# Moving one modulation block of layer 1 from the first attention to the handover behind the first expert stage

## The chip, the cores and the metric

The kernel runs on one core of a Trainium2 chip as one launch. The metric is the device time of that launch in microseconds (us). Three runs of the kernel before took 3518.69, 3520.12 and 3525.53 us; the median is 3520.12. TensorE (PE) multiplies matrices, VectorE (DVE), ScalarE (ACT) and GpSimd (POOL) do elementwise work, SyncE (SP) issues most of the transfers (DMAs).

## What is computed

Two transformers of two layers each run one behind the other on 512 tokens of width 1024 (and 256 context tokens in the first). All numbers are float32. Of the first:

```python
for l in range(2):
    mod_l = silu(c) @ w_ada[l] + b_ada[l]            # 6 x 1024 numbers; mod_c likewise from c_ctx
    sh1, sc1, g1, sh2, sc2, g2 = split(mod_l, 6)
    h = rmsnorm(x, norm_mix[l]) * (1 + sc1) + sh1    # ctx likewise, with mod_c
    o = mixer_ab(h) if l == 0 else mixer_na(h)       # two kinds of attention
    x = x + g1 * o
    h = rmsnorm(x, norm_ffn[l]) * (1 + sc2) + sh2
    x = x + g2 * hier_moe(h)                         # 32 experts, each token goes to 2
x = rmsnorm(x, norm_final)                           # then the second transformer
```

The modulation vectors depend on `c` and `c_ctx` alone, so each can be computed at any time before its first use. A modulation block here is 2048 columns of one layer's `w_ada`. Block (1, 1) is columns 2048 to 4095 of layer 1: the gate `g1` and the shift `sh2`. Both are first used behind layer 1's attention (called NA).

## The kernel before, in words

Stages run in this order: start and projections, the first attention, its output projection and the router, the first expert stage, the first handover, the norm and turn of the NA input, the NA attention, the second expert stage, the second handover, and the second transformer. A scheduler places instructions in each engine's queue; an engine works through its queue strictly in that order, and a weight load takes the next slot of a ring (`wraw`, a 512 KB load issued by SP). A slot is free again when its last reader is done.

**Modulation blocks.** `ada_pieces(l, b, ...)` gives eight steps, k = 0 to 7. Each issues two 512 KB loads of `w_ada` and four matmuls, one for each quarter of the columns, which add into one PSUM bank `ad` (L405); `cc` is the silu of `c` and `c_ctx`. A matmul in float32 shows as two records in the trace. Behind step 7, DVE adds the bias and POOL writes the result to the buffer `mod` with two DMAs. Five blocks (two of layer 0, three of layer 1) make 40 steps, which `mixer_ab` spreads evenly over the 96 groups of the first attention.

**Expert stage.** `moe` and `experts` run 32 experts one after another. An expert's weights are 12 loads (gate and up 8, down 4). Its tokens are transposed (L1284), multiplied by gate and up (`ex_in`, L1275, `ea<-wr,xT`), passed through the activation (`sg`, L1297 and L1298), transposed again (L1308), copied out by DVE (`aT`, L1309), multiplied by down (L1275, `ea<-wr,aT`), scaled on DVE by the token's weight and gain (`ey`, L1319 and L1320) and scattered to the buffer `Y` by POOL (L1321). `ex_arms` is the branch that does this for 64 tokens, or for 128 if the expert has more. L1319 in layer 0 writes `ey`, so it waits until the earlier scatter that reads the same buffer has landed.

**Overflow block.** An expert with more tokens than 128 gets a further block. With these inputs one such block runs in layer 0 and none in layer 1. `overflow` issues its 12 loads from inside the loop, then the first loads of the next stage (`then`, here `na_w_in`); the block itself runs behind the loop (L1146 and L1147), and behind it a loop for still more blocks (L1149) that doesn't run.

**Handover.** `gains` spreads a row of gains over 128 partitions (`spread`, L441 and L442), 32 records on PE in layer 0; before, this stands ahead of the overflow block. Then ACT loads a function table and casts the next stage's weights (`wh<-wr`), SP loads the rows of `Y` (`yp`), and for each tile DVE adds them into `xO`, ACT and DVE form the normed `h`, and PE transposes it. `warm` is a run of matmuls whose result nobody reads; `warm(ps, xO[:, 0, 0:512], 6)` stands at the first tile of the first handover, one on `xO[:, 2]` in the second handover.

Of the kernel before, what the change touches and what calls it, by code (L numbers as in the profile page):

```python
# [8 lines left out]
F32 = mybir.dt.float32  # L9
# [5 lines left out]
ALU = mybir.AluOpType  # L15
# [4 lines left out]
P = 128  # L20
# [46 lines left out]
class Ker:  # L67
# [320 lines left out]
    def ada_pieces(self, l, b, ap, ps, tag, keep=None):  # L388

        nc = self.nc  # L390
        c0 = b * 2048
        g = {}

        def tile(k):
            if k == 0:
                g["a"] = ps.tile([P, 512], F32, name="ad", tag=tag, bufs=3 if tag == "pt" else None)
                g["b"] = ap.tile([P, 512], F32, name="adab", tag="adab", bufs=1)
                nc.gpsimd.memset(g["b"], 0.0)
                for who in range(2):
                    nc.gpsimd.dma_start(self.quarters(g["b"], who), self.I["b_ada"][l, c0:c0 + 2048].rearrange("(j n) -> j n", j=4))  # L400
# [6 lines left out]
            if k == 7:  # L407
                nc.vector.tensor_add(g["b"], g["b"], g["a"])
                if keep is not None:
                    keep.append(g["b"])  # L410
                    return
                for who in range(2):
                    nc.gpsimd.dma_start(self.mod[l, who, c0:c0 + 2048].rearrange("(j n) -> j n", j=4), self.quarters(g["b"], who))
        return [lambda k=k: tile(k) for k in range(8)]
# [171 lines left out]
    def mixer_ab(self, xO, begin=None):  # L586
# [8 lines left out]
        with ExitStack() as eo:  # L595
# [139 lines left out]
            with ExitStack() as e3:  # L735
# [105 lines left out]
                for b in range(3):  # L841
                    ada += self.ada_pieces(1, b, pp, ps, "pt")
# [13 lines left out]
            with ExitStack() as e1:  # L856
                pp = e1.enter_context(self.pool(name="abp", bufs=1))
                ps = e1.enter_context(self.pool(name="abps6", bufs=3, space=PSUM))
                self.weights(e1, 8, 0, "right")
# [221 lines left out]
    def moe(self, l, xO, t0, nt, who_of, sc=None, then=()):  # L1081
# [12 lines left out]
        with ExitStack() as e1:  # L1094
# [14 lines left out]
            pg = e3.enter_context(self.pool(name=f"mg{l}", bufs=1, side="right"))  # L1109
            px = e1.enter_context(self.pool(name=f"mx{l}", bufs=2, side="right"))  # L1110
            ps = e1.enter_context(self.pool(name=f"mqs{l}", bufs=8, space=PSUM))
# [23 lines left out]
            def overflow():  # L1135
# [8 lines left out]
            nov, w = self.experts(l, tix, idx, wl, ctx, xg, hD, Y, T, px, ps,  # L1144
                                  [first] + past + ([] if l else [self.shift_scale]), gains, overflow)
# [155 lines left out]
    def ex_out(self, w, sg, h, idx, wl, Y, T, px, ps):  # L1301
# [30 lines left out]
    def experts(self, l, tix, idx, wl, ctx, xg, hD, Y, T, px, ps, past, gains, overflow):  # L1332
# [6 lines left out]
        a = ps.tile([P, 512], F32, name="ea", tag="b")  # L1339
        self.ex_in(a, w, x, 0, range(2))  # L1340
        for e in range(NE):
# [13 lines left out]
            if e + 1 < NE:  # L1355
                a = ps.tile([P, 512], F32, name="ea", tag="b")
                self.ex_in(a, w1, x1, 0, range(2))
# [4 lines left out]
        gains()  # L1362
# [35 lines left out]
    def table(self, fn):  # L1398

        t = self.sm.tile([P, 1], F32, name="tab")  # L1400
# [10 lines left out]
    def mixer_na(self, xO, begin=None, finish=None):  # L1411
# [13 lines left out]
        with ExitStack() as e1:  # L1425
# [3 lines left out]
            with ExitStack() as e2:  # L1429
# [23 lines left out]
                with ExitStack() as e3:  # L1453
                    ps = e3.enter_context(self.pool(name="naps", bufs=8, space=PSUM))
# [3 lines left out]
                    with self.pinned():  # L1458
# [32 lines left out]
                        for t in range(NT + 2):  # L1491
# [4 lines left out]
                            if add and t == 0:  # L1496
                                self.warm(ps, xO[:, 0, 0:512], 6)
# [127 lines left out]
            with ExitStack() as e2:  # L1625
                self.halves(e2, 8, "right")
# [110 lines left out]
    def even_mixer(self, xO, normed=False, finish=None):  # L1737
# [3 lines left out]
        with ExitStack() as e1:  # L1741
            OT = xO[:, 4:6, :].rearrange("p a (b n) -> p (a b) n", n=512)
            with ExitStack() as e2:
# [8 lines left out]
                with ExitStack() as e3:  # L1752
# [46 lines left out]
                    else:  # L1799
# [6 lines left out]
                        self.warm(ps, xO[:, 2, 0:512], 6)  # L1806
# [141 lines left out]
    def conv_ffn(self, l, xO, dst=None):  # L1948
        nc, tc, I = self.nc, self.tc, self.I
        wu, wd = I["ffn_w_up_2"][l], I["ffn_w_down_2"][l]  # L1950
        with ExitStack() as e1:
            ph = e1.enter_context(self.pool(name=f"ff{l}", bufs=1))
# [362 lines left out]
```

## Time and profile before

| | us |
|---|---|
| median of three runs | 3520.12 |
| the profiled execution | 3519.27 |
| its span | 3517.5 |
| mean granted clock of TensorE | 0.977 |
| first attention, 200 to 490: PE busy | 283.57 |
| first expert stage, 612 to 1150: PE busy | 496.25 |
| first handover, 1150 to 1213: PE busy | 37.54 |
| second handover, 2140 to 2220: PE busy | 67.53 |

The span is the time between the first and the last instruction of the profile; 1.77 us of the profiled time lie around it. [...] In a row of a timeline, what stands in brackets is the idle time of the engine ahead of it and what ended it.

### The profile page before, as it was taken

How to read it: one execution, taken by the hardware profiler on the slowest of the kernel's cores; microseconds unless marked ns; L12 is line 12 of the kernel's file. 1: busy time of each engine (PE TensorE's matmuls, PEld its weight loads, DVE VectorE, ACT ScalarE, POOL GpSimd, SP SyncE). 2: the span in 40 equal slices, each digit the busy share in tenths (PEclk: the TensorE clock that was granted, in tenths of full speed). 3: DMA queues.
4: the chain of work that ended last, by engine and by line, in shares of the span. 5: the costliest groups of instructions: out<-in, count | busy, mean ns of one | idle time of the engine just before them, and what ended most of it. 6: DMA issues, size and time to landing. Idle time of an engine off the chain costs nothing. (4 is left out here: it accounts for less than half of the span.)

```text
span 3517.5 us, 44393 instructions
## 1 busy us (share of the span) xinstructions
PE 3270.0 (93%) x16460; PEld 2118.1 (60%) x16460; DVE 1515.1 (43%) x2899; ACT 1027.7 (29%) x1908; POOL 468.3 (13%) x569
## 2 busy tenths in 40 slices
PE   7999998999988699998988888998999999999998
PEld 5954556333322387765332234876888888788887
DVE  3476565222222356565211114527443456455344
ACT  3475541100000144441000002326332334333232
POOL 1044421111111023331111110103000000000000
PEclk9999999999999899999999999999999999999999
DMA  5134465798999622236999996322333354233331
GB/s 202 49 119 133 166 217 196 306 417 329 352 410 397 229 73 75 69 113 226 416 408 399 402 397 244 122 91 85 96 96 96 84 66 95 70 99 105 96 97 48
DMA packets 350859, 676.34 MB, mean 192 GB/s; under 512 B 42804, under 2 KB 194548, under 8 KB 349184
## 3 DMA queue, kind: packets, MB, share of 16 engines
q1 hardware_dynamic: 313816, 626.50, 50.6%
q0 software_dynamic: 17360, 25.94, 2.1%
q10 hardware_dynamic: 19416, 20.34, 1.8%
q8 instruction: 168, 2.75, 0.3%
q14 instruction: 99, 0.81, 0.1%
HBM read 676.22 MB, written 29.19 MB: 201 GB/s over the span
## 5 line engine op out<-in xcount | busy, mean ns | idle before, releaser
L1275 PE MATMUL ea<-wr,xT 128*64 128x512 f32 x2336 | 607.5, 601 | 38.5 <-DMA wr<-in_moe_w_up_dram 21.8
L157 DVE TENSOR_TENSOR wh<-wr,wh 128x1024 fp32r<-128x1024 f32 (+2 forms) x269 | 328.8, 1228 | 308.9 <-ACT wh L156 308.2
L240 PE MATMUL aw<-hh,wh 128*128 128x512 f32 (+1 forms) x1184 | 432.1, 366 | 2.9 <-ACT wh L156 2.6
L241 PE MATMUL aw<-hl,wh 128*128 128x512 f32 (+1 forms) x1184 | 432.7, 366 | 0.0
L242 PE MATMUL aw<-hh,wh 128*128 128x512 f32 (+1 forms) x1184 | 431.4, 365 | 0.0
L1275 PEld LDWEIGHTS ea<-wr,xT 128*64 128x64 f32 x2336 | 178.9, 137 | 408.9 <-issue 293.5
L156 ACT CAST wh<-wr 128x1024 fp32r<-128x1024 f32 (+2 forms) x269 | 274.2, 1027 | 417.6 <-PE acc L242 287.4
L1275 PE MATMUL ea<-wr,aT 128*64 128x512 f32 x1168 | 284.4, 632 | 53.0 <-DVE aT L1309 43.5
L240 PEld LDWEIGHTS aw<-hh,wh 128*128 128x128 f32 x1184 | 223.9, 189 | 39.7 <-ACT wh L156 3.5
L241 PEld LDWEIGHTS aw<-hl,wh 128*128 128x128 f32 x1184 | 224.3, 189 | 38.3 <-issue 3.5
L242 PEld LDWEIGHTS aw<-hh,wh 128*128 128x128 f32 x1184 | 224.1, 189 | 37.6 <-issue 3.5
L510 POOL TENSOR_TENSOR pp<-pp,rc 128x768 f32<-128x768 f32 (+3 forms) x192 | 211.0, 1106 | 260.0 <-DVE rc L509 247.3
L1285 ACT COPY xT<-pt 128x512 f32<-128x512 f32 x65 | 38.1, 586 | 683.8 <-PE pt L1284 672.9
L1275 PEld LDWEIGHTS ea<-wr,aT 128*64 128x64 f32 x1168 | 82.7, 144 | 200.1 <-issue 136.6
L1321 POOL DMA_INDIRECT Y<-ey,idx x73 | 73.1, 1001 | 848.3 <-DVE ey L1320 767.2
L508 ACT ACTIVATE pp<-s,nm 128x768 f32<-128x768 f32 (+3 forms) x192 | 137.1, 716 | 157.4 <-DVE nm L1593 81.1
L240 PE MATMUL acc<-wh,hh 128*128 128x512 f32 (+2 forms) x480 | 177.8, 370 | 0.0
L241 PE MATMUL acc<-wh,hh 128*128 128x512 f32 (+2 forms) x480 | 176.4, 368 | 0.0
L242 PE MATMUL acc<-wh,hl 128*128 128x512 f32 (+2 forms) x480 | 176.1, 367 | 0.0
L1297 ACT ACTIVATE sg<-ea 64x256 f32<-64x256 f32 x146 | 54.9, 376 | 302.4 <-PE ea L1275 237.7
L241 PE MATMUL acc<-wh,ah 128*128 128x512 f32 x352 | 137.8, 392 | 0.0
L1298 DVE TENSOR_TENSOR sg<-sg,ea 64x256 f32<-64x256 f32 x146 | 62.0, 425 | 175.7 <-ACT sg L1297 173.0
(493 smaller groups left out, 5166.5 us busy)
## 6 DMA issues: line engine op xcount, KB each, us to landing
wr<-in_moe_w_gate_dram SPq DMA_DIRECT2D x260, 512.0 KB
wr<-in_moe_w_up_dram SPq DMA_DIRECT2D x260, 512.0 KB
wr<-in_moe_w_down_dram SPq DMA_DIRECT2D x260, 512.0 KB
wr<-in_w_ada_dram SPq DMA_DIRECT2D x96, 512.0 KB
wr<-in_ffn_w_up_dram SPq DMA_DIRECT2D x88, 512.0 KB
wr<-in_ffn_w_down_dram SPq DMA_DIRECT2D x44, 512.0 KB
wr<-in_odd_w_in_dram SPq DMA_DIRECT2D x32, 512.0 KB
wr<-in_na_w_in_dram SPq DMA_DIRECT2D x30, 512.0 KB
```

The source lines that it names most:

```text
L156: keep(self.nc.scalar.copy(hi, raw))
L157: keep((self.lo_eng or self.nc.vector).tensor_sub(lo, raw, f(hi)))
L240: mm(ps, ah, bh, start=first, stop=False)
L241: mm(ps, ah, bl, start=False, stop=False)
L242: mm(ps, al, bh, start=False, stop=last)
L508: nc.scalar.activation(p[:, :n], s[:, b:b + n], AF.Exp, bias=nm, scale=sign, accum_out=rc)
L510: nc.gpsimd.tensor_mul(p[:, :n], p[:, :n], rc.broadcast_to([P, n]))
L1275: self.tc.keep_in_program_order(self.nc.tensor.matmul(*a, **k))
L1285: (self.nc.vector.tensor_copy if g else self.nc.scalar.copy)(x[:, g * 4:g * 4 + 4, :], pt.rearrange("p (k t) -> p k t", t=P))
L1297: self.nc.scalar.activation(sg[64:, c], a[:64, c], AF.Silu)
L1298: self.nc.vector.tensor_mul(sg[64:, c], sg[64:, c], a[64:, c])
L1321: nc.gpsimd.indirect_dma_start(Y.rearrange("t (h d) -> (t h) d", h=2), bass.IndirectOffsetOnAxis(ap=idx[:, h], axis=0), y, None, bounds_ch ...
```

## The change

- Block (1, 1) is no longer among the first attention's steps; four blocks, 32 steps, are spread over the same 96 groups. `ada_load` issues the two loads of a step, and `ada_pieces` can be given loads that are already issued.
- In `moe` of layer 0, `overflow` issues the loads of steps 0 and 1 behind those of `na_w_in`, in slots 16 to 19 of the ring's 32; the 12 others are issued in the program behind `experts`. The eight steps stand behind the overflow block, with a PSUM bank of their own. The end (bias and writes to `mod`) runs at the third tile of the NA norm.
- `gains` runs behind the overflow block in both layers.
- The L1319 instruction of before keeps its place in program order, behind the copy `aT`.
- `warm` at the first tile of the first handover is gone; that of the second handover reads the final gain `gfin` and has nine matmuls instead of six.
- PSUM banks in the expert stage: `ea` of the input products has two of its own, the others share five (layer 0) or six. NA's `naps` goes from eight to seven. Some pads in SBUF keep later buffers in place; the tile of `table` shares a name with another.

```diff
+    def ada_load(self, l, b, k):
+        return [self.wraw(self.I["w_ada"][l, k * P:(k + 1) * P, c:c + 1024]) for c in (b * 2048, b * 2048 + 1024)]
...
-            for half in range(2):
-                raw = self.wraw(self.I["w_ada"][l, k * P:(k + 1) * P, c0 + half * 1024:c0 + half * 1024 + 1024])
+            for half, raw in enumerate(raws[k] if raws else self.ada_load(l, b, k)):
...
-                for b in range(3):
+                for b in (0, 2) if begin else range(3):
                     ada += self.ada_pieces(1, b, pp, ps, "pt")
...
                 self.raws = [self.wraw(s) for s in then]
+                if ada:
+                    self.n = RING + 11
+                    self.ada_raws = [self.ada_load(1, 1, k) for k in range(2)]
                 return nov, w
...
+            if ada:
+                self.ada_raws += [self.ada_load(1, 1, k) for k in range(2, 8)]
             with tc.If(nov > 0):
                 self.ex_block(w, xo, slots, px, ps, nc.values_load(tix[64:65, NE:NE + 1], min_val=0, max_val=int(BIG)))
+            gains()
+            if ada:
+                *steps, self.ada_end = self.ada_pieces(1, 1, pg, pad, "b", raws=self.ada_raws)
+                for p in steps:
+                    p()
...
-            nc.vector.scalar_tensor_tensor(y, self.dgain, ctx[:, h], self.gain, ALU.mult, ALU.add)
+            self.tc.keep_in_program_order(
+                nc.vector.scalar_tensor_tensor(y, self.dgain, ctx[:, h], self.gain, ALU.mult, ALU.add))
...
-                            if add and t == 0:
-                                self.warm(ps, xO[:, 0, 0:512], 6)
+                            if add and t == 2:
+                                self.ada_end()
...
-                        self.warm(ps, xO[:, 2, 0:512], 6)
+                        self.warm(ps, self.gfin[:, 0:512], 9)
```

PE at the end of the first expert stage, before: the output arm of expert 31, the gain spreads (`mrow`), then the overflow block (its transposes of `xg_5787` and its products).

```order
L1376 UNCONDITIONAL_BRANCH
L1139 COMPARE_AND_BRANCH
...
L1308 MATMUL pt<-c_ident,sg 128x64 x4
L1275 MATMUL ea<-wr,aT 64x512 x8
L1376 UNCONDITIONAL_BRANCH
L441 MATMUL mrow<-nA,c_ident 128x128 x16
L1146 COMPARE_AND_BRANCH
L1147 TENSOR_LOAD tix
L1284 MATMUL pt<-c_ident,xg_5787 128x128 x8
L1275 MATMUL ea<-wr,xT 64x512 x16
```

The same place after; `ad` is the block that was moved, four matmuls to a step.

```order
L1295 MATMUL ea<-wr,xT 64x512 x5
L409 MATMUL ad<-wr,cc 32x512 x4
...
L1328 MATMUL pt<-c_ident,sg 128x64 x4
L1295 MATMUL ea<-wr,aT 64x512 x8
L1396 UNCONDITIONAL_BRANCH
L409 MATMUL ad<-wr,cc 32x512 x12
L1161 COMPARE_AND_BRANCH
...
L448 MATMUL mrow<-nA,c_ident 128x128 x16
L409 MATMUL ad<-wr,cc 32x512 x8
L1169 COMPARE_AND_BRANCH
...
L409 MATMUL ad<-wr,cc 32x512 x8
```

Step 0 now stands between the input products of expert 31 and its output arm, steps 1 to 3 between that arm and the overflow block, the spreads and steps 4 and 5 behind the block, and steps 6 and 7 ahead of the first transposes of the NA norm.

SP behind the overflow block's loads, before: the first loads of `na_w_in`, the branches of the arms, the block and the loop behind it, then the loads of `Y`.

```order
L144 DMA wr<-in_na_w_in_dram 128x4x256 x2
L144 DMA wr<-in_na_w_in_dram 128x8x128
L1359 TENSOR_LOAD tix
L1359 ISA x2
L144 DMA wr<-in_na_w_in_dram 128x8x128
...
L1146 COMPARE_AND_BRANCH
...
L1149 UNCONDITIONAL_BRANCH
L52 DMA yp<-Y_5611 128x2048 x5
```

The same place after.

```order
L144 DMA wr<-in_na_w_in_dram 128x4x256 x2
L144 DMA wr<-in_na_w_in_dram 128x8x128
L144 DMA wr<-in_w_ada_dram 128x1024 x4
...
L144 DMA wr<-in_w_ada_dram 128x1024 x7
L1161 COMPARE_AND_BRANCH
...
L144 DMA wr<-in_w_ada_dram 128x1024 x3
L1169 COMPARE_AND_BRANCH
...
L144 DMA wr<-in_w_ada_dram 128x1024 x2
L144 DMA wr<-in_na_w_in_dram 128x8x128 x2
L52 DMA yp<-Y_5544 128x2048 x6
```

The sixteen loads of `w_ada` now stand between `na_w_in` and `yp`, and two loads of `na_w_in`, of which the second goes into a slot that a cast of DVE has to free, stand directly ahead of `yp`.

## Rows read from the trace of the kernel before

**Rows 1.** Stretches: us, busy us (records) of each engine, clock, DMA share, GB/s.

```profile
200.00:490.00 290.00, 283.57 (x1632) 143.01 (x1630) 185.47 (x380) 166.58 (x383) 142.95 (x146) 1.00 0.46 152
...
612.00:1150.00 538.00, 496.25 (x2313) 175.10 (x2312) 132.91 (x256) 49.05 (x109) 67.83 (x68) 0.98 0.95 369
1150.00:1213.00 63.00, 37.54 (x154) 15.63 (x152) 18.57 (x24) 9.02 (x15) 2.92 (x3) 0.81 0.63 237
...
2140.00:2220.00 80.00, 67.53 (x384) 45.90 (x381) 41.90 (x51) 26.09 (x43) 19.14 (x25) 0.91 0.57 190
```

**Rows 2.** Modulation: stretch of its tile alone (PE, PEld, DVE), then PE's timeline.

```profile
203.00:490.00 287.00, 68.65 (x320) 9.86 (x320) 3.40 (x5) 1.00 0.47 154
...
307.06 1.07 PE L405 MATMUL ad<-wr,cc 128*32 128x512 f32 x8
308.06 0.70 PE L813 MATMUL s<-qka 96*128 96x256 f32 x2
...
312.18 1.06 PE L405 MATMUL ad<-wr,cc 128*32 128x512 f32 x6
```

**Rows 3.** PE's timeline through the first handover: start, us, operation.

```profile
1159.89 0.34 PE L1308 MATMUL pt<-c_ident,sg 64*128 64x64 f32 x2 [0.47 <-DVE sg L1298]
1166.63 5.00 PE L1275 MATMUL ea<-wr,aT 128*64 128x512 f32 x16 [6.40 <-issue]
1171.57 3.83 PE L441 MATMUL mrow<-nA,c_ident 32*128 32x128 f32 x32
1175.33 1.09 PE L1284 MATMUL pt<-c_ident,xg 128*128 128x128 f32 x8
1176.72 7.09 PE L1275 MATMUL ea<-wr,xT 128*64 128x512 f32 x32 [0.29 <-ACT xT L1285]
...
1187.11 5.00 PE L1275 MATMUL ea<-wr,aT 128*64 128x512 f32 x16 [1.17 <-DVE aT L1309]
1205.55 7.78 PE L52 MATMUL warm<-xO,c_ident 128*128 128x512 f32 x12 [13.43 <-DVE xO L52]
1213.16 0.22 PE L52 MATMUL pt<-nsel,nparts 96*128 96x128 bf16 x1
```

**Rows 4.** DVE's timeline in the first handover.

```profile
1165.32 0.75 DVE L1319 SCALAR_TENSOR_TENSOR ey<-dgain,ctx,gain 128x512 f32<-128x512 f32 x1 [5.48 <-DMA Y<-ey,idx]
...
1207.19 1.29 DVE L52 SCALAR_TENSOR_TENSOR h<-xO,ss,xg 128x1024 f32<-128x1024 f32 x1
```

**Rows 5.** SP's queue in the first handover.

```profile
1157.60 4.00 SPq L144 DMA_DIRECT2D wr<-in_moe_w_down_dram  x4
1167.82 4.07 SPq L144 DMA_DIRECT2D wr<-in_na_w_in_dram  x4
1198.01 8.97 SPq L52 DMA_DIRECT2D yp<-Y  x5
```

**Rows 6.** Stretches of 5 us in the first handover, columns as in rows 1.

```profile
1165.00:1170.00 5.00, 3.37 (x10) 1.27 (x12) 1.18 (x2) 0.00 (x0) 0.00 (x0) 0.56 0.66 239
1170.00:1175.00 5.00, 5.00 (x38) 3.75 (x35) 1.44 (x2) 1.04 (x2) 0.97 (x1) 1.00 0.97 298
1175.00:1180.00 5.00, 4.71 (x28) 2.27 (x28) 1.39 (x2) 0.72 (x2) 0.00 (x0) 1.00 0.42 140
```

**Rows 7.** ACT's table load and DVE's first weight casts behind the overflow block.

```profile
1192.63 1.28 ACT L52 ACT_TABLE_LOAD   x1 [7.53 <-PEq L1149]
...
1195.09 3.50 DVE L52 TENSOR_TENSOR wh<-wr,wh 128x1024 fp32r<-128x1024 f32 x3 [2.17 <-ACT wh L52]
```

**Rows 8.** The second handover: PE's warm run and transposes, DVE's add, one stretch.

```profile
2171.28 7.81 PE L52 MATMUL warm<-xO,c_ident 128*128 128x512 f32 x12 [4.97 <-issue]
2184.28 1.94 PE L52 MATMUL pt<-c_ident,fh 128*128 128x128 f32 x8 [5.20 <-DVE fh L52]
...
2179.12 1.23 DVE L52 TENSOR_TENSOR xO<-xO,yp 128x1024 f32<-128x1024 f32 x1 [1.86 <-PE warm L52]
...
2185.00:2190.00 5.00, 4.86 (x22) 4.22 (x21) 4.31 (x6) 2.35 (x4) 0.59 (x2) 0.50 1.00 334
```

More of the change, by code (lines that the diff above doesn't have):

```diff
@@ L386, in ada_block, with ada_pieces @@
             p()
-    def ada_pieces(self, l, b, ap, ps, tag, keep=None):
+    def ada_load(self, l, b, k):
+        return [self.wraw(self.I["w_ada"][l, k * P:(k + 1) * P, c:c + 1024]) for c in (b * 2048, b * 2048 + 1024)]
+    def ada_pieces(self, l, b, ap, ps, tag, keep=None, raws=None):
         nc = self.nc
@@ L406, in tile, with end @@
                                      start=k == 0, stop=k == 7)
[L407 to L414, printed above, removed]
+            if k == 7 and not raws:
+                end()
+        def end():
+            self.nc.vector.tensor_add(g["b"], g["b"], g["a"])
+            if keep is not None:
+                keep.append(g["b"])
+                return
+            for who in range(2):
+                nc.gpsimd.dma_start(self.mod[l, who, c0:c0 + 2048].rearrange("(j n) -> j n", j=4), self.quarters(g["b"], who))
+        return [lambda k=k: tile(k) for k in range(8)] + ([end] if raws else [])
     def quarters(self, t, i):
@@ L858, in mixer_ab @@
                 ps = e1.enter_context(self.pool(name="abps6", bufs=3, space=PSUM))
+                self.pad(e1, 192, "right")
                 self.weights(e1, 8, 0, "right")
@@ L1109, in moe @@
             pg = e3.enter_context(self.pool(name=f"mg{l}", bufs=1, side="right"))
+            ada = then and l == 0
+            pad = e3.enter_context(self.pool(name=f"mad{l}", bufs=1, space=PSUM, side="right")) if ada else None
             px = e1.enter_context(self.pool(name=f"mx{l}", bufs=2, side="right"))
-            ps = e1.enter_context(self.pool(name=f"mqs{l}", bufs=8, space=PSUM))
+            ps = e1.enter_context(self.pool(name=f"mqs{l}", bufs=5 if ada else 6, space=PSUM))
             xg = [pg.tile([P, D], F32, name=f"xg{i}", tag=f"xg{i}") for i in range(3)]
@@ L1142, in overflow @@
                 self.raws = [self.wraw(s) for s in then]
+                if ada:
+                    self.n = RING + 11
+                    self.ada_raws = [self.ada_load(1, 1, k) for k in range(2)]
                 return nov, w
             nov, w = self.experts(l, tix, idx, wl, ctx, xg, hD, Y, T, px, ps,
-                                  [first] + past + ([] if l else [self.shift_scale]), gains, overflow)
+                                  [first] + past + ([] if l else [self.shift_scale]), overflow)
+            if ada:
+                self.ada_raws += [self.ada_load(1, 1, k) for k in range(2, 8)]
             with tc.If(nov > 0):
                 self.ex_block(w, xo, slots, px, ps, nc.values_load(tix[64:65, NE:NE + 1], min_val=0, max_val=int(BIG)))
+            gains()
[3 more added lines that the diff above has]
+                    p()
             self.n = RING + 11
@@ L1330, in ex_rest, with experts @@
         self.ex_out(w, sg2, 1, *out)
-    def experts(self, l, tix, idx, wl, ctx, xg, hD, Y, T, px, ps, past, gains, overflow):
+    def experts(self, l, tix, idx, wl, ctx, xg, hD, Y, T, px, ps, past, overflow):
         nc = self.nc
@@ L1338, in experts @@
         w = self.ex_load_w(l, 0)
-        a = ps.tile([P, 512], F32, name="ea", tag="b")
+        a = ps.tile([P, 512], F32, name="ea", tag="ea", bufs=2)
         self.ex_in(a, w, x, 0, range(2))
@@ L1355, in experts @@
             if e + 1 < NE:
-                a = ps.tile([P, 512], F32, name="ea", tag="b")
+                a = ps.tile([P, 512], F32, name="ea", tag="ea", bufs=2)
                 self.ex_in(a, w1, x1, 0, range(2))
@@ L1398, in table @@
     def table(self, fn):
-        t = self.sm.tile([P, 1], F32, name="tab")
+        t = self.sm.tile([P, 1], F32, name="ss")
         self.nc.scalar.activation(t, self.eps[EPS], fn)
@@ L1453, in mixer_na @@
                 with ExitStack() as e3:
-                    ps = e3.enter_context(self.pool(name="naps", bufs=8, space=PSUM))
+                    ps = e3.enter_context(self.pool(name="naps", bufs=7 if finish else 8, space=PSUM))
                     nA, parts, sel = self.nmod
@@ L1625, in mixer_na @@
             with ExitStack() as e2:
+                self.pad(e2, 352, "right")
                 self.halves(e2, 8, "right")
@@ L1951, in conv_ffn @@
         with ExitStack() as e1:
+            if l:
+                self.pad(e1, 192)
             ph = e1.enter_context(self.pool(name=f"ff{l}", bufs=1))
```

1 line of the change is left out of this document (removed).

## The prediction

> **What bounds the kernel now.** I read the stretch table first [rows 1]. In the first attention (200 to 490 us) TensorE (PE) is busy 283.57 of 290.00 us at full clock; every other engine has a third of the time free. Work taken off PE there shortens the stage. The expert loop (612 to 1150) is bound by weights: DMA share 0.95. Between them and the next stage lies the first handover (1150 to 1213), where PE is busy 37.54 of 63.00 us and the clock is 0.81: there a chain of waits sets the time, and what is put into it must be placed on that chain. The second handover (2140 to 2220) is of the same kind, smaller.
>
> Then I followed the first handover row by row. PE has transposed expert 31's activations by 1160.2. Then it stands 6.40 us, because VectorE (DVE) waits 5.48 us for an older scatter into Y at L1319, ahead of the copy aT that PE wants [rows 3, 4]. Output product of 31 at 1166.63, gain spreads (L441, 3.83 us) at 1171.57, then the overflow block from 1175.33 to 1192.11, a second block of one expert's tokens with its own 12 weight loads. After it ScalarE loads a table and casts weights, SyncE (SP) issues the loads of Y (yp) at 1198.01, h is ready at 1208.48, and PE runs the warm matmuls from 1205.55 until the first transposes at 1213.16: 4.7 us after h was there [rows 3 to 5, 7].
>
> **Part 1, the attention: a loss of PE work.** The five modulation blocks cost 68.65 us for 320 records [rows 2], two records to a matmul, so 160 matmuls and 13.73 us a block. Four matmuls go to four column groups side by side: a round of eight records takes 1.07 us and the next work begins 1.00 us after it began, and a part of a round, six records with other work between, takes 1.06 [rows 2]. In the order of before I count 65 rounds and parts of rounds, after the change 52. 13 x 1.00 = **-13.0 us**. Bounds: -13.7 (a block's busy time) and -6.5 (if the 6.43 us that PE now idles in the stage doubled; nothing there shows which engine would do that, since DVE is busy 185.47 and ScalarE 166.58 of 290).
>
> **Part 2, where the eight k-steps land: PE stands and waits.** The order of after has step k0 ahead of the output arm of expert 31, and k1 to k3 ahead of the overflow block; PE works strictly through that order. The loads of k0 are on SP behind the overflow block's 12 loads and three of na_w_in. In the trace SP is held after the twelve until 1167.82, and then issues four na_w_in in 4.07 us, 1.02 each [rows 5]. DMA was still at 0.97 and 298 GB/s in 1170 to 1175, and at 0.42 of the next 5 us, so the fourth load had landed about 1177.1 [rows 6]. One load of 512 KB at 298 GB/s takes 1.76 us. k0 needs two loads behind three, five in all: 1177.1 + 1.76 = 1178.9. Its four matmuls, PE having stood 19 us: twice a round, 2.1; to 1181.0. Now the arm of 31: two pairs of transposes at 0.34, then the copy aT and its latencies as ahead of the overflow block's output product, 1.17, then the product at 4.5, a little under the 5.00 that it takes after a stand [rows 3]; to 1187.3. The 6.40 us stand of before is inside this wait and isn't paid twice. k1 lies ready. k2 and k3 go into slots that expert 31's own weights held, which PE gives back as it enters that arm, about 1181: four loads x 1.76 + about 1.2 from first issue, to 1189.3, and k3's round after that: the overflow block begins at about 1190.4. Before, it began at 1175.33 [rows 3]: **+15.1 us**. The gain spreads, which stood ahead of it, are now behind it, which is in this number.
>
> Bounds of part 2: if k0's loads came as early as the arm of 31, the stand would vanish, with it the 6.40 (the copy aT is now ahead of the waiting instruction of DVE), and the block would begin at 1175.33 - 6.40 - 3.83 + 4 x 1.0 = 1169.1: -6.2. The upper bound: k2 and k3 released only when the arm of 31 ends, 6.3 us later: +21.4. I take the worked value, since the order fixes both queues and the rows give the rates.
>
> [...]
>
> **Part 3, behind the block.** Call PE's end of the block T (1192.11 before). Before: table load T + 0.52, first DVE weight cast T + 2.98, yp issue T + 5.90, h T + 16.37, transposes T + 21.05 [rows 3 to 5, 7]. After: the spreads (3.83) and k4, k5 (two rounds, 2.1) stand between T and the signal on which ScalarE begins: +5.9 for the table load and the casts. In SP's order a na_w_in load that needs the slot of the first DVE cast now stands ahead of yp: cast begins T + 8.9, ends T + 10.1, the load's issue 1.0, yp issued T + 11.1, that is 5.2 later than before; h ready T + 21.6. The warm matmuls at this place are gone, so the transposes begin then: T + 21.8, against T + 21.05: **+0.7 us**. Bounds: -4.7 (the whole warm run, if yp isn't held) and +2 (transposes at half clock, 1.94 for eight [rows 8], on the first two tiles). k6, k7 and the end (one DVE add, two POOL transfers at the third tile) run beside waits; the add on DVE in front of a later h is at most a full-width copy, 0.7: I take +0.3. POOL has nothing queued behind it that this stage waits for.
>
> **Part 4, the second handover.** The warm matmuls read xO and DVE's add into xO waits 1.86 us for them [rows 8]. After, they read the final gain, and that wait is gone; nine instead of six at 0.65 end about 2181.7, below the first transposes, which then begin near 2182.4 at a higher clock than the 0.50 of 2185 to 2190. **-2.5 us**; bounds -4 and 0 (if the casts ahead of the first products set the pace anyway).
>
> Pads, the table tile's name and PSUM buffers (eight to seven in tiles; five or six plus two for ea): 0, covered by an expert loop that the weights bound (PE is free 42 of 538 us [rows 1]); without that cover a wait for a bank would cost about what PE waits for a copy out of one, 1.17 us [rows 3], at each place.
>
> **The sum.** -13.0 + 15.1 + 0.7 + 0.3 - 2.5 = +0.6 us on the profiled 3519.27 us, which is 0.85 below the median of the runs: 3519.9. I say **3520 us**, no change that can be measured (this kernel's measurement can tell 0.2%, 7 us, so "same" is 3513 to 3527).
>
> **Rivals.** (A) The loads are there in time, so that PE doesn't stand at k0: the step's matmuls fill the wait that was idle anyway. Then part 2 is -6.2 and the sum is -13.0 - 6.2 + 0.7 + 0.3 - 2.5 = -20.7: 3499 us. [...] For it: DMA is nearly idle after 1177 [rows 6], so there is room if SP gets to issue early. Against: SP is held to 1167.82 behind the twelve loads, and the order puts na_w_in ahead.
>
> (B) Slower: the slots of k2 and k3 come free only at the end of expert 31's output arm, so PE stands a second time ahead of the overflow block: part 2 is +21.4, and a second stand leaves the block's 32 input matmuls (7.09 us at full clock [rows 3]) at half clock for their first half, +3.5. Sum -13.0 + 21.4 + 3.5 + 0.7 + 0.3 - 2.5 = +10.4: 3530 us. It decides from a release 4 us later than I worked out. For it: the clock row of 1165 to 1170 shows 0.56 right after the 6.40 us stand. Against: those slots hold weights which the input products alone read.
>
> (C) PE's freed time in the attention isn't a gain, because the softmax engines set the pace once PE has room: -6.5 instead of -13.0, 3526 us, on the edge of slower. Against: [rows 1].
>
> **How the numbers follow.** My forecast 0.40, its own range 3513 to 3527. A 0.32, most of it between 3499 and 3512. B 0.22. C 0.06, half of it slower. Faster is A, and a little of the forecast's lower side: 0.33. Slower is B, half of C and a little of the upper side: 0.27. Same: 0.40. The range leaves out the far end of A and what lies beyond B: 3500 to 3532.
>
> **What would show it.** The attention's stretch shorter by 12 to 13 us with 256 records at L409. In the first handover a PE wait of some 17 to 19 us ahead of the first four matmuls of L409, released by the DMA of w_ada; the overflow block some 15 us later than expert 31 would put it. No wait of the copy aT on Y. First transposes about 22 us after the block. In the second handover no wait of DVE on warm. I'm wrong if the PE wait at k0 is below 10 us, if k2 or k3 show a wait of over 4 us of their own, or if yp is issued less than 8 or more than 14 us after the block.

## The result, and the profile after

The changed kernel takes **3537.79 us** (five runs, 3534.29 to 3546.54) against 3520.12 us before: ratio 1.0051, 95% interval 1.0040 to 1.0062. It is 17.7 us slower. I had said 3520 us, with a range up to 3532, and "slower" had the smallest chance of the three. The forecast was wrong. The profiled execution took 3537.73 us (span 3535.7, mean granted clock 0.973 of full speed).

**Where the time went.** The same instruction is looked up in the profiled execution of each kernel. The table gives its start before and the difference from that in other kernels; e6, e9 and e12 are experiments told below. `ey` is DVE's last step on an expert's tokens (L1320 before, L1341 after).

| start of | before, us | after | e6 | e9 | e12 |
|---|---|---|---|---|---|
| first expert's `ey`, first stage | 632.3 | -13.7 | -10.9 | +3.3 | -12.7 |
| expert 30's `ey` | 1157.6 | -19.4 | -24.7 | +2.5 | -24.1 |
| overflow block's `ey` | 1192.2 | +2.0 | -3.9 | +3.5 | -29.8 |
| first transposes of `h` | 1213.2 | +5.5 | -2.9 | +3.5 | -22.1 |
| first `ey`, second stage | 1663.2 | +7.4 | +0.9 | +4.6 | -16.1 |
| last `ey`, second stage | 2164.4 | +17.0 | +3.2 | +5.5 | -15.5 |
| second handover, first transposes | 2184.3 | +14.4 | +0.9 | +4.8 | -17.7 |
| last PE instruction | 3505.5 | +18.1 | +1.6 | +3.8 | -17.2 |

Read the column "after" downward. The kernel is 13.7 us ahead behind the first attention and 19.4 us ahead at expert 30. By the first transposes of `h` it is 5.5 us behind. The second expert stage, in which the diff changes nothing but PSUM banks and addresses, costs another 9.6 us. Of the rest, the NA attention costs 1.9, the second handover gives back 2.6, and the second transformer loses 3.7.

The attention by the stretch table and by the moved tile (columns as in rows 1 and 2; the DMA share is the mean busy share of the 16 DMA engines): 256 records instead of 320, and PE busy 54.66 us instead of 68.65.

```profile
200.00:490.00 290.00, 272.88 (x1574) 142.84 (x1572) 188.70 (x387) 172.61 (x390) 140.73 (x140) 0.98 0.40 132
...
1138.00:1220.00 82.00, 41.90 (x199) 15.47 (x196) 17.09 (x23) 9.02 (x15) 2.91 (x3) 0.75 0.72 265
```

```profile
203.00:490.00 287.00, 54.66 (x256) 8.03 (x256) 2.67 (x4) 0.98 0.41 134
```

From expert 30's `ey` to the first transposes of `h` it is now 80.5 us; before it was 55.6. The stretch cut out for the handover holds 41.90 us of PE work in 82 us, before 37.54 in 63 [rows 1]. PE's timeline there, answering to rows 3 (start, length, line, operation; in brackets the idle time ahead and what ended it):

```profile
1137.99 3.60 PE L1295 MATMUL ea<-wr,xT 128*64 128x512 f32 x14
1163.34 2.97 PE L409 MATMUL ad<-wr,cc 128*32 128x512 f32 x8 [21.75 <-DMA wr<-in_w_ada_dram]
1166.24 0.46 PE L1328 MATMUL pt<-c_ident,sg 64*128 64x64 f32 x4
1167.28 3.65 PE L1295 MATMUL ea<-wr,aT 128*64 128x512 f32 x16 [0.58 <-DVE aT L1329]
1170.86 1.91 PE L409 MATMUL ad<-wr,cc 128*32 128x512 f32 x12
1173.15 1.05 PE L409 MATMUL ad<-wr,cc 128*32 128x512 f32 x4 [0.38 <-DMA wr<-in_w_ada_dram]
1174.51 1.05 PE L409 MATMUL ad<-wr,cc 128*32 128x512 f32 x4 [0.30 <-DMA wr<-in_w_ada_dram]
1176.56 1.05 PE L409 MATMUL ad<-wr,cc 128*32 128x512 f32 x4 [1.00 <-DMA wr<-in_w_ada_dram]
1177.55 1.09 PE L1304 MATMUL pt<-c_ident,xg 128*128 128x128 f32 x8
...
1188.74 5.35 PE L1295 MATMUL ea<-wr,aT 128*64 128x512 f32 x16 [0.58 <-DVE aT L1329]
1194.02 4.85 PE L448 MATMUL mrow<-nA,c_ident 32*128 32x128 f32 x32
1198.80 3.64 PE L409 MATMUL ad<-wr,cc 128*32 128x512 f32 x16
1202.65 2.39 PE L409 MATMUL ad<-wr,cc 128*32 128x512 f32 x16 [0.20 <-PEq L1169]
...
1218.70 0.80 PE L52 MATMUL pt<-c_ident,h 128*128 128x128 f32 x2 [13.50 <-DVE h L52]
```

PE has the input products of expert 31 behind it at 1141.6 and then stands 21.75 us, because the next instruction in its queue is step k0 and the load of `w_ada` has not landed. The output arm of expert 31, which wants nothing but PE, stands behind it. SP's queue and ACT's table load (rows 5 and 7):

```profile
1153.01 2.85 SPq L144 DMA_DIRECT2D wr<-in_na_w_in_dram  x3
1156.85 29.62 SPq L144 DMA_DIRECT2D wr<-in_w_ada_dram  x16
1186.52 20.56 SPq L144 DMA_DIRECT2D wr<-in_na_w_in_dram  x2
1207.32 16.11 SPq L52 DMA_DIRECT2D yp<-Y  x6
```

```profile
1202.99 1.28 ACT L52 ACT_TABLE_LOAD   x1 [5.21 <-PEq L1169]
```

In the second handover the add no longer waits for the warm matmuls: DVE's adds follow one another, and the transposes of `fh` begin 2.6 us earlier against the last `ey` than before (rows 8 have 1.86 us of wait there). The eight transposes still take 1.97 us; before they took 1.94 [rows 8].

```profile
2193.07 1.22 DVE L52 TENSOR_TENSOR xO<-xO,yp 128x1024 f32<-128x1024 f32 x1
...
2198.70 1.97 PE L52 MATMUL pt<-c_ident,fh 128*128 128x128 f32 x8 [5.42 <-DVE fh L52]
```

The second expert stage, by the stretch table of before and of after (PE, PEld, DVE, ACT, POOL, then clock, DMA share, GB/s):

```profile
1720.00:1920.00 200.00, 178.39 (x784) 63.03 (x781) 35.34 (x65) 17.40 (x39) 26.38 (x26) 0.96 1.02 408
```

```profile
1720.00:1920.00 200.00, 171.85 (x779) 61.88 (x776) 35.31 (x65) 17.41 (x39) 25.95 (x26) 0.94 1.02 399
```

The DMA engines are busy all the time in both (share 1.02), yet they move 399 GB/s instead of 408: the same full queues carry 2% less.

### The profile page after: what moved, and what is told of

Same layout as the page of the kernel before. It is cut to its first block, busy times and chain, and to the rows that moved or that the text cites. A ratio compares the mean times of both kernels' runs of the same rounds, so it can differ in the third digit from the quotient of the medians.

```text
span 3535.7 us, 44403 instructions
## 1 busy us (share of the span) xinstructions
PE 3264.5 (92%) x16454; PEld 2120.6 (60%) x16454; DVE 1510.4 (43%) x2899; ACT 1029.8 (29%) x1910; POOL 469.7 (13%) x569
## 5 line engine op out<-in xcount | busy, mean ns | idle before, releaser
L240 PE MATMUL aw<-hh,wh 128*128 128x512 f32 (+1 forms) x1184 | 432.9, 367 | 1.8 <-ACT wh L156 1.3
L240 PEld LDWEIGHTS aw<-hh,wh 128*128 128x128 f32 x1184 | 224.6, 190 | 38.4 <-ACT wh L156 2.4
L240 PE MATMUL acc<-wh,hh 128*128 128x512 f32 (+2 forms) x480 | 177.2, 369 | 0.0
L1329 DVE COPY aT<-pt 128x256 f32<-128x256 f32 x73 | 30.9, 423 | 273.4 <-PE pt L1328 273.4
```

The source lines that it names most:

```text
L240: mm(ps, ah, bh, start=first, stop=False)
```

## The experiments

Two questions were open: what the eight steps cost where they stand, and why a stage that the diff hardly touches moves its weights more slowly. Medians are of each kernel's runs; a ratio is against runs of the kernel before on the same chip, with its 95% interval. The rates in the expectations are medians of short stretches; the measured ones are means of 200 us and lie some 5 GB/s lower.

### The PSUM banks: e1, e2

e1 is the changed kernel with the second expert stage's banks as they were:

```diff
-            ps = e1.enter_context(self.pool(name=f"mqs{l}", bufs=5 if ada else 6, space=PSUM))
+            ps = e1.enter_context(self.pool(name=f"mqs{l}", bufs=5 if ada else 8, space=PSUM))
...
-        a = ps.tile([P, 512], F32, name="ea", tag="ea", bufs=2)
+        a = ps.tile([P, 512], F32, name="ea", tag="b" if l else "ea", bufs=None if l else 2)
...
```

> The changed kernel with the second expert stage's PSUM banks as before (eight shared, input products without banks of their own), which puts nine instead of ten input products ahead of the next transposes there. Theory P (the banks moved one pair of products, so PE stands 1.03 instead of 0.18 us behind each expert and its clock falls in every second one): the second expert stage is 9 to 11 us shorter than in the changed kernel, an expert takes 14.4 us again, about 3527 us. Rival R (the loads of that stage ran slower for another reason, such as where buffers lie): still 3536 to 3539 us.

Measured: 3537.2 us, ratio 1.0051 (1.0034 to 1.0068), no better than the change. PE's order within an expert went back to that of before, but 1720 to 1920 still shows 401 GB/s at share 1.02. The banks are not why the weights are slow.

e2 is the kernel before with nothing but the new banks in `experts` (two for `ea`, six for the others):

```diff
-            ps = e1.enter_context(self.pool(name=f"mqs{l}", bufs=8, space=PSUM))
+            ps = e1.enter_context(self.pool(name=f"mqs{l}", bufs=6, space=PSUM))
...
-        a = ps.tile([P, 512], F32, name="ea", tag="b")
+        a = ps.tile([P, 512], F32, name="ea", tag="ea", bufs=2)
...
```

> The kernel before with only the PSUM change of both expert stages (two banks for the input products, six for the rest). Theory P: the second expert stage is 9 to 11 us longer, the first within 4 us, about 3530 us. Rival R: 3518 to 3523 us.

Measured: 3543.86 us, 1.0067 (1.0050 to 1.0084). In the profile the first expert stage is 14.1 us longer, the handover 6.6 and the second stage 3.9 (406 GB/s there). The stretch table of the first stage:

```profile
612.00:1150.00 538.00, 480.14 (x2256) 169.71 (x2257) 129.40 (x251) 47.24 (x106) 67.01 (x67) 0.97 0.92 359
```

Before it was 0.95 and 369 GB/s [rows 1]. This stage isn't held by the weights alone: with other banks PE does less in the same time and the DMA engines idle more. So the price of banks here isn't hidden. PE's waits between 640 and 1130 us name the place (what waits, on what: us in total, times, longest):

```profile
PE pt L1284 <- ACT xT L1285: 17.9, 23, 1.8
```

By the profile PE stands between the two halves of an expert's transposes until ACT has copied out the first. The kernel before and e6 show no such wait in that stretch.

### The small edits: e4

The kernel before, with the order of DVE's `ey` instruction kept and the second warm run changed:

```diff
-            nc.vector.scalar_tensor_tensor(y, self.dgain, ctx[:, h], self.gain, ALU.mult, ALU.add)
+            self.tc.keep_in_program_order(
+                nc.vector.scalar_tensor_tensor(y, self.dgain, ctx[:, h], self.gain, ALU.mult, ALU.add))
...
-                        self.warm(ps, xO[:, 2, 0:512], 6)
+                        self.warm(ps, self.gfin[:, 0:512], 9)
```

> The kernel before with only two of the edits: the gain instruction of DVE kept behind the copy aT, and the second handover's warm run on the final gain with nine matmuls. Expected from the trace of the changed kernel: second handover 4 us shorter (DVE does not wait for the warm run), the first expert stage up to 3 us shorter and no 5.48 us wait of DVE ahead of expert 31's copy: 3510 to 3516 us in all. If these were not what shortened those stretches: 3518 to 3522.

Measured: 3512.89 us, 0.9981 (0.9971 to 0.9991): 6.3 us faster than the kernel before on the same chip. In the profile it is 2.4 us ahead at expert 30's `ey` and 7.8 at expert 31's. DVE's timeline at expert 31 shows why. The wait for `Y` is still there, 4.59 us, but it now stands behind the copy `aT` that PE wants (rows 4 have it ahead):

```profile
1157.91 0.42 DVE L1309 COPY aT<-pt 128x256 f32<-128x256 f32 x1 [0.49 <-PE pt L1308]
1162.92 0.75 DVE L1320 SCALAR_TENSOR_TENSOR ey<-dgain,ctx,gain 128x512 f32<-128x512 f32 x1 [4.59 <-DMA Y<-ey,idx]
```

The second handover, for which I had expected 4 us, gave 1.1.

### Where the steps stand: e3

The changed kernel, with the matmuls of the eight steps held to program order, so that all stand behind the overflow block:

```diff
-                    nc.tensor.matmul(g["a"][j * 32:j * 32 + 32, :], self.ada_c[:, k, :], raw[:, q * 512:q * 512 + 512],
...
+                    i = nc.tensor.matmul(g["a"][j * 32:j * 32 + 32, :], self.ada_c[:, k, :], raw[:, q * 512:q * 512 + 512],
...
+                    if raws:
+                        self.tc.keep_in_program_order(i)
```

> The changed kernel with all eight steps of the moved block held behind the overflow block on PE. Theory S (the stand of 21.75 us ahead of step 0 is what the first handover lost): no stand, the overflow block ends some 25 us earlier, then the transfers of w_ada and Y set the pace, so 15 to 21 us of it are won, about 3517 to 3523 us. Rival D (the transfers ahead of Y on SP's queue set the end of the handover anyway): yp is issued as late as in the changed kernel, within 5 us, 3533 us or more.

Measured: 3517.04 us, 0.9991 (0.9980 to 1.0001): 20.8 us below the changed kernel. PE no longer stands; expert 31's output arm, the block, the spreads and the first six steps follow one another:

```profile
1148.57 3.65 PE L1297 MATMUL ea<-wr,aT 128*64 128x512 f32 x16 [0.59 <-DVE aT L1331]
1153.13 1.06 PE L1306 MATMUL pt<-c_ident,xg 128*128 128x128 f32 x8 [0.90 <-PE ea L1297]
...
1169.32 3.93 PE L450 MATMUL mrow<-nA,c_ident 32*128 32x128 f32 x32
1173.18 3.78 PE L409 MATMUL ad<-wr,cc 128*32 128x512 f32 x24
```

The block begins 24.4 us earlier than in the changed kernel, the first transposes of `h` only 16.3. The difference goes back in a later table load on ACT and later loads of `Y`: both come 21.5 us behind the end of the block's last products, against 8.9 and 13.2. ACT idles 17.91 us ahead of the table load, until SP leaves the branch behind the block (L1171); e7 shows what SP stood for at that branch. The second stage still runs at 399 GB/s.

### The address of the ring's slots: e5, e6, e9, e8, e10, e11

The tile of `table` had a name of its own, `tab`, and now shares the name `ss`. So its pool is smaller, and every buffer allocated behind it lies 192 bytes lower, the 32 slots of the weight ring among them. By the addresses of the built kernels a slot begins at byte 256 modulo 512 of a partition before, and at 64 after; the added pads stand elsewhere and don't undo this. e5 is the kernel before with the renamed tile alone; apart from bare semaphore waits, the instructions of every engine and their order are the same.

```diff
-        t = self.sm.tile([P, 1], F32, name="tab")
+        t = self.sm.tile([P, 1], F32, name="ss")
```

> The kernel before with one edit: the tile of table() takes the name ss, which frees 192 bytes a partition and moves every later buffer 192 bytes down, so the ring's weight slots lie 64 instead of 256 bytes behind a multiple of 512; the order of PE, SP, DVE and POOL is the same. Theory A (where a slot lies sets the rate of the weight loads): median rate in the second expert stage 404 to 406 instead of 412 GB/s, that stage 6 to 9 us longer, about 3528 to 3534 us. Rival P (the PSUM banks slowed the stage): 3518 to 3522 us.

Measured: 3536.22 us, 1.0045 (1.0028 to 1.0061): **15.9 us for a name**, a little more than Theory A had.

e9 is e5 with a pad of 192 bytes ahead of the ring, which puts the slots, and what is allocated behind them, back where they were:

```diff
+        self.pad(es, 192)
         self.ring = es.enter_context(self.pool(name="ring", bufs=RING))
```

> The kernel before with the tile of table() named ss, and a pad of 192 bytes a partition ahead of the ring, which puts the ring and all behind it back to where the kernel before has them. Theory A (the place of the weight slots): the 16 us that the name cost are gone, 3517 to 3523 us and 412 GB/s. Rival N (sharing the name itself, its small buffers or their waits, costs the time): 3533 us or more.

Measured: 3520.83 us, 0.9990 (0.9981 to 1.0000). The loss is gone. The stretch 1720 to 1920 of e5 and of e9:

```profile
1720.00:1920.00 200.00, 178.53 (x774) 62.84 (x772) 34.55 (x64) 17.40 (x39) 25.64 (x26) 0.95 1.02 400
```

```profile
1720.00:1920.00 200.00, 178.45 (x796) 63.34 (x794) 36.58 (x68) 18.11 (x41) 26.37 (x26) 0.97 1.02 408
```

The DMA queues of 1700 to 1900 say the same in another view (packets, MB, share of 16 engines), before and e5: the same share of time, 1.5% less moved.

```profile
q1 hardware_dynamic: 21478, 78.22, 97.5%
```

```profile
q1 hardware_dynamic: 21162, 77.05, 97.5%
```

e8, e10 and e11 leave the name as it was and put a pad of 256, 64 or 128 bytes ahead of the ring of the kernel before:

```diff
+        self.pad(es, 256)
```

> The kernel before with 256 bytes a partition of pad ahead of the ring: the slots begin at a multiple of 512 bytes, all else in the same order. Theory A with finer places still better: rate above 412 GB/s and 5 us or more won, under 3515 us. If 256 is as good as 512: 412 GB/s and 3517 to 3522 us.

> The kernel before with a pad of 64 bytes a partition ahead of the ring: slots 320 bytes behind a multiple of 512. If a place at a multiple of 256 bytes is what counts: 404 to 406 GB/s and 3530 to 3538 us, as with 64 bytes. If the cost of the name was a low address or anything else: 412 GB/s and 3517 to 3523 us.

> The kernel before with a pad of 128 bytes a partition ahead of the ring: slots 384 bytes behind a multiple of 512. If multiples of 128 bytes suffice: 412 GB/s, 3517 to 3523 us. If only multiples of 256 do: 404 to 406 GB/s, 3530 to 3538 us.

| kernel | slot begins at, mod 512 | GB/s, 1720 to 1920 | median us | ratio |
|---|---|---|---|---|
| before | 256 | 408 | 3520.12 | |
| e9 | 256 | 408 | 3520.83 | 0.9990 |
| e8 | 0 | 407 | 3520.56 | 1.0002 |
| e5 | 64 | 400 | 3536.22 | 1.0045 |
| e10 | 320 | 401 | 3538.35 | 1.0040 |
| e11 | 384 | 401 | 3539.92 | 1.0040 |

```profile
1720.00:1920.00 200.00, 176.28 (x764) 61.64 (x760) 34.61 (x64) 16.81 (x38) 25.42 (x25) 0.95 1.02 401
```

That line is e10's. Of the places tried, the multiples of 256 bytes (0 and 256) are equally good, and 64, 320 and 384 are equally bad. The packets themselves show it: in 1720 to 1920 a packet of 4096 bytes took 162.3 to 162.6 ns on average in the kernel before, e8 and e9, and 164.6 to 165.2 ns in e5, e10 and e11. That is the rate. How much of the 15 to 17 us comes by it is less clear, since each of these edits moves every buffer behind the ring as well. In the profiled executions of e5, e10 and e11, which are 19 to 22 us longer than that of the kernel before, 7 to 9 us lie in the two expert stages.

e6 is the changed kernel with the old name, and nothing else:

```diff
-        t = self.sm.tile([P, 1], F32, name="ss")
+        t = self.sm.tile([P, 1], F32, name="tab")
```

> The changed kernel with the tile of table() under its old name, so the ring's slots lie as in the kernel before. Theory A: rate 412 GB/s again in both expert stages, 7 to 12 us shorter than the changed kernel, 3526 to 3531 us. Rival P: 3535 to 3540 us.

Measured: 3526.04 us, 1.0016 (1.0006 to 1.0025), 11.8 us below the changed kernel; 407 GB/s in 1720 to 1920. The stand at step k0 is still there, 5.9 us earlier:

```profile
1132.72 3.60 PE L1295 MATMUL ea<-wr,xT 128*64 128x512 f32 x14
1157.45 3.37 PE L409 MATMUL ad<-wr,cc 128*32 128x512 f32 x8 [21.13 <-DMA wr<-in_w_ada_dram]
...
1171.69 1.09 PE L1304 MATMUL pt<-c_ident,xg 128*128 128x128 f32 x8
```

### Both mended: e7, e12

e7 is the changed kernel with the old name and the eight steps behind the loop that follows the block, kept in order (the steps' own lines unchanged, moved down):

```diff
-            if ada:
-                *steps, self.ada_end = self.ada_pieces(1, 1, pg, pad, "b", raws=self.ada_raws)
...
-            self.n = RING + 11
+            self.n = RING - 1 if ada else RING + 11
...
+            if ada:
+                *steps, self.ada_end = self.ada_pieces(1, 1, pg, pad, "b", raws=self.ada_raws)
...
+            self.n = RING + 23
...
```

> The changed kernel with the old name, and the moved block's steps behind the branch that follows the overflow block, so that PE stands for none of them and ScalarE's table load does not wait for them. Theories S and A together: handover 20 us and expert stages 7 to 12 us shorter than in the changed kernel: 3503 to 3511 us. If the transfers ahead of Y set the handover's end instead, 3515 us or more.

Measured: 3506.49 us, 0.9954 (0.9937 to 0.9971). Now ACT's table load and SP's loads of `Y` wait for the branch of that loop. SP comes to it at 1169.96 us, with its 14 loads of `w_ada` ahead of it issued, the last at 1169.59, and then waits 9.3 us on the branch's own line (the second row, of SP's waits: us in total, times, longest). That last load landed at 1179.72, and at 1179.73 SP went on. At the same branch SP's wait ended at 1185.03 in the changed kernel and at 1177.51 in the kernel before, where the last of the weight loads issued ahead of it landed at 1185.01 and 1177.49.

```profile
1180.60 1.28 ACT L52 ACT_TABLE_LOAD   x1 [11.54 <-SPq L1167]
...
SPq L1167 <- SPq L1167: 9.7, 2, 9.3
```

e12 adds the banks of before in the second stage, and the program issues half of the sixteen loads inside `overflow` and half behind the branch:

```diff
-                    self.ada_raws = [self.ada_load(1, 1, k) for k in range(2)]
+                    self.ada_raws = [self.ada_load(1, 1, k) for k in range(4)]
...
-            if ada:
-                self.ada_raws += [self.ada_load(1, 1, k) for k in range(2, 8)]
...
+            if ada:
+                self.n = RING + 19
+                self.ada_raws += [self.ada_load(1, 1, k) for k in range(4, 8)]
```

> The changed kernel with the old name of the table tile, the second expert stage's PSUM banks as before, the steps of the moved block behind the branch that follows the overflow block, and one instead of two loads of na_w_in ahead of Y. The kernel e7 took 3506.5 us; the banks should give back 2 us, the earlier Y load 1 to 3: 3500 to 3505 us. If SP's hold for all transfers ahead of that branch sets the handover's end: 3504 to 3508 us.

Measured: **3504.19 us**, 0.9943 (0.9923 to 0.9962): faster than the kernel before and than the changed one; its interval overlaps e7's, so it isn't told apart from e7. The time lies in both ranges that I had given. The wait at the branch is hardly shorter, because the edit didn't do what it was for: the scheduler moved loads ahead of the branch, and on SP's queue 14 of the 16 stand ahead of it, as in e7. The last of them landed at 1175.61, and SP went on at 1175.63.

```profile
1176.49 1.28 ACT L52 ACT_TABLE_LOAD   x1 [10.57 <-SPq L1165]
...
SPq L1165 <- SPq L1165: 10.4, 2, 9.9
```

What is gained when fewer loads are out at the branch was therefore not tried.

## Why the prediction was wrong, and where it was right

The terms of the sum beside the same stretches of the profiled executions of after and of e6, which is after with its ring where it was. Each number is a difference of two rows of the first table.

| stretch | predicted | after | e6 |
|---|---|---|---|
| part 1, up to the first `ey` | -13.0 | -13.7 | -10.9 |
| first expert stage, to expert 30 | 0 | -5.7 | -13.8 |
| parts 2 and 3, to the transposes of `h` | +15.8 | +24.9 | +21.8 |
| NA attention, to the second stage | +0.3 | +1.9 | +3.8 |
| second expert stage | 0 | +9.6 | +2.3 |
| part 4, second handover | -2.5 | -2.6 | -2.3 |
| second transformer | 0 | +3.7 | +0.7 |
| sum | +0.6 | +18.1 | +1.6 |

Against the forecast the changed kernel has 17.5 us too much: 9.6 in the second expert stage, 3.7 in the second transformer, 3.4 in the first expert stage and the first handover taken together, 1.6 in the NA attention, less 0.8 in parts 1 and 4.

**The step that failed** is the one-line term "Pads, the table tile's name and PSUM buffers (...): 0, covered by an expert loop that the weights bound". The signs that I had named for being wrong all lay in the handover, and none of them came; they couldn't have shown this. The term failed in three points.

First, the reason given was the wrong way round for the table tile's name. It has no work that could be covered, but it moves the ring, and in e5, e8, e9, e10 and e11 the weights' rate goes with the ring's address. If the weights bound a stage, then a slower weight transfer isn't covered by that stage; it is that stage's time. e5 shows this edit alone at +15.9 us and e9 undoes it. In the changed kernel, taking it back is worth 11.8 us (e6), and e6's 3526 us lies inside the forecast's own range of 3513 to 3527. I had read the added pads as keeping later buffers in place and did not look at the addresses.

Second, the cover itself was misread for the first expert stage. Its DMA share of 0.95 looks like a bound, but it moves 369 GB/s [rows 1] where the second stage moves 408 at share 1.02. That leaves 1 - 369/408 = 10% of 538 us in which more could have been moved. e2 loses 14.1 us in that stage by banks alone, and with them come 17.9 us of PE waiting for ACT's copy `xT`. e6 gains 13.8 with the same two banks for `ea`, five others instead of six, and DVE's `ey` kept in order. DVE's order alone, in e4, moves the stage by 1.3 us. In e6 that wait is absent, and in the rows read there PE has two records of input products ahead of an expert's transposes. Which of e6's edits makes the difference was not tried.

Third, the banks weren't free in the second stage either, but they cost little there: +2.3 in e6, +3.9 in e2 and +4.1 in e7, against +0.6 in e12, which has the banks of before.

**Part 1 was right**: -13.7 and -10.9 in the two profiles, against -13.0 and the end of -6.5 that rival C took. The softmax engines did not take the pace over. (A single profile scatters here: e9, which changes nothing in this stage, has +3.3.)

**Part 2's mechanism was right, and its size only in the changed kernel as it was.** I had PE standing some 17 to 19 us at k0, released by the DMA of `w_ada`: 21.75. I had the block 15.1 us late in a frame shifted by part 1. It began at 1177.55 instead of 1175.33, 2.2 us later; with the 13.7 us of part 1 that is 15.9. But in e6 the same difference is 1171.69 - 1175.33 + 10.9 = 7.3. The loads of k0 come behind the loop's last weights. That they would land behind the three of `na_w_in` I had assumed; no row that I had read showed it. In the changed kernel they did: the three landed at 1158.18, 1159.66 and 1161.26, k0's two at 1163.30 and 1164.43. With the 13.7 us of part 1 the last is 1178.1, against the forecast's 1178.9. The loop's faster work and its slower weights nearly cancel there, so the loads land where I had put them. The agreement is partly luck. PE's own lead at expert 30 is worth nothing as long as k0 waits: after is 19.4 us ahead there and e6 24.7, and both lose all but what the loads allow. k0's eight records took 2.97 us at a granted clock of 0.53, against the 2.1 that I had put, twice a round. k1 to k3 showed no long wait (0.38, 0.30 and 1.00 us ahead of the later ones), so rival B, the second stand, did not come; nor did A, since the loads were late as worked out.

**Part 3 was right in its waits, and undersized in the changed kernel**: +3.6 instead of +0.7. The block's last products end at T = 1188.74 + 5.35 = 1194.09. The table load came at T + 8.9 instead of T + 6.4: the spreads took 4.85 us, not 3.83, and k4 and k5 3.64, not 2.1. `yp` was issued at T + 13.2, not T + 11.1, and the first transposes began at T + 24.6, not T + 21.8. The granted clock is what had been left out. It was 0.66 over the spreads and steps; in e6, where it was 1.00, they took 3.93 and 1.92 us, the table load came at T + 6.3, `yp` at T + 10.6 and the transposes at T + 22.1, all within 0.6 us of the forecast (the stretch of after, then of e6, columns as in rows 1):

```profile
1194.00:1203.00 9.00, 8.79 (x54) 5.36 (x56) 2.13 (x3) 1.18 (x3) 0.98 (x1) 0.66 0.02 6
...
1188.00:1196.00 8.00, 7.79 (x66) 4.62 (x64) 2.13 (x3) 2.67 (x5) 0.97 (x1) 1.00 0.05 13
```

The first transposes then ran at a granted clock of 0.50, 0.80 us for the first two records, after PE had idled 13.50 us and with no warm run ahead of them; before, behind the warm run, it was 1.00 and 0.44 us.

**Part 4 was right in size, partly by luck**: -2.6 against -2.5. The wait of 1.86 us is gone, as worked out. The higher clock didn't come: it was 0.50 over the eight transposes, which took 1.97 us, before 0.50 and 1.94. In its place DVE's first weight cast began 5.85 us behind the last `ey` instead of 7.11, which I hadn't forecast. In e4, which has this edit without the later `gains`, the handover gave 1.1 us. The sum had a slip too: nine matmuls are eighteen records, which at 0.65 us each would end at 2183.0 and not 2181.7. They took 7.96 us, so it cost nothing.

**What the change was worth without the stand and the moved ring** is e12: 18.9 us below the kernel before on the same chip (3523.09). That is more than parts 1 and 4 together, since e12 also gains 11.4 us in the first expert stage, and less than it could be, since SP still waits 9.9 us at the branch for its loads.

**Left open.** The last 3.7 us of the changed kernel, in the second transformer (0.7 in e6). PE idles as long there as before (47.8 us, before 47.5) and is busy 3.4 us longer; the granted clock is at 0.50 for 50.1 us between the first transposes of `fh` and the end of the span, before for 36.2. e10 and e11, with 53 us at 0.50, lose 7.5 and 10.7 us behind the second stage. The place of the slots is not the cause: e1 and e3, with slots at 64, are 2.6 and 2.4 us shorter than the kernel before in this stretch. The clock isn't all of it either: e9, with 45.4 us at 0.50, is 1.0 us shorter. Why the clock fell was not tried. And the table's sums are those of single executions: e6's profiled one took 3520.82 us, 5.2 below the median of its runs, so its small entries (1.9, 2.3, 3.8 us) are not settled to better than that.

## What to carry to other kernels

A renamed, resized or padded buffer moves every buffer behind it (by 192 bytes here): list the addresses of the DMA destinations before and after a diff, and keep those on a stage's bound at multiples of 256 bytes, the places that were good here (405 to 408 GB/s over all the kernels, at the other places 399 to 401). Ask of every term set at zero which resource covers it, and whether the edit slows that very resource; and compare GB/s, not the busy share, to see whether a stage is at the transfer's limit (399 and 408 GB/s both stood at a share of 1.02 here). Work moved into an idle stretch goes behind what doesn't need its data: an engine that works its queue in order turns one early instruction with a late operand into a stand for all that follows (21.75 us ahead of k0). When an edit is meant to move instructions, look in the built order whether it did.

## What the runs showed of the hardware that I had not expected

**The weight loads ran about 2% slower when their slots began 64 or 128 bytes behind a multiple of 256.** In 1720 to 1920 full queues moved 407 to 408 GB/s with slots at 0 or 256 modulo 512 (before, e8, e9), and 400 to 401 with slots at 64, 320 or 384 (e5, e10, e11); a packet of 4096 bytes took 162.3 to 162.6 ns in the former and 164.6 to 165.2 in the latter. Other distances were not tried. The loss did not grow with the distance: e10 and e11 (64 and 128 behind a multiple of 256) both show 401 GB/s. It is the written side of the loads that these edits moved. What makes such a load slower was not shown.

**PE's products did not slow with the slots' place.** In the second transformer the products of L240 took these times over the whole trace (records, then busy us and mean ns) in the kernel before, in e5 and in the changed kernel, whose slots lie at 256, 64 and 64:

```profile
L240 PE MATMUL acc<-wh,ah 128*128 128x512 f32 x352 | 137.5, 390 | 0.0
...
L240 PE MATMUL acc<-wh,ah 128*128 128x512 f32 x352 | 138.1, 392 | 0.0
...
L240 PE MATMUL acc<-wh,ah 128*128 128x512 f32 x352 | 136.9, 389 | 0.0
```

e6, with slots at 256, shows 392. So these differences of a few ns don't explain what e5, e10 and e11 lose behind the second stage (3.7, 7.5 and 10.7 us).

**At a branch ACT stood until SP's loads had landed.** In e7 ACT waited 11.54 us at the branch for SP, in e12 10.57. In e7 SP had reached it 10.6 us before ACT's table load began, and went on 0.01 us after the last load that it had issued ahead of it had landed (1179.72 and 1179.73); in e12 it was 0.02 us (1175.61 and 1175.63). No data of these loads was wanted by ACT.
